# Half-size filling parcels in a stick-breaking attention mixer, and two down products in one PSUM bank

## The chip, the cores and the metric

The kernel runs on one core of one Trainium2 chip. The metric is device time of one execution in microseconds (us); lower is better. The engines are TensorE (PE, its weight loads PEld), VectorE (DVE), ScalarE (ACT), GpSimd (POOL) and SyncE (SP), which issues most loads.

## What is computed

A decoder trunk of two layers on 512 tokens with width 1024. Each layer is a half-step SwiGLU FFN (width 2816), a mixer, and a second half-step FFN, each behind an RMSNorm. Layer 0's mixer is a gated linear attention (GLA); layer 1's is stick-breaking attention with 16 heads of width 64, which the change's short name calls the softmax mixer:

```python
def sb_mixer(h, w_in, w_out):                      # per 128-query block, per head
    q, k, v = jnp.split(h @ w_in, 3, axis=-1)
    ...
        z = jnp.einsum('bhtd,bhsd->bhts', q_blk, k).astype(jnp.float32) * scale
        sp = jnp.where(mask, jax.nn.softplus(z), 0.0)
        rem = lax.cumsum(sp, axis=3, reverse=True) - sp
        weights = jnp.where(mask, jnp.exp(jax.nn.log_sigmoid(z) - rem), 0.0)
        return jnp.einsum('bhts,bhsd->bhtd', weights.astype(v.dtype), v)
    ...
    return o @ w_out
for i in range(DEPTH):
    x = x + 0.5 * swiglu(rmsnorm(x, ffn1_norm[i]), ffn1_w_gate[i], ffn1_w_up[i], ffn1_w_down[i])
    h = rmsnorm(x, mix_norm[i])
    y = gla_mixer(h, ...) if i % 2 == 0 else sb_mixer(h, ...)
    x = x + y
    x = x + 0.5 * swiglu(rmsnorm(x, ffn2_norm[i]), ffn2_w_gate[i], ffn2_w_up[i], ffn2_w_down[i])
return rmsnorm(x, final_norm)
```

## The kernel before

All activations stay on the chip, features on the 128 partitions, the 512 tokens along the free axis. Every weight is loaded as float32 (tile `raw` or `rawd`), split by ScalarE into a rounded high part `wh` (L129) and by VectorE into the rest `wl` (L130); the inputs are split in the same way. A product is then three matmuls (high by high, low by high, high by low; `mm3`, L66).

**The feed.** All weight products of the program stand in one list of entries in order (`Feed`, L140). `start()` begins the next entry; it also splits the weights of the entries that follow and issues loads up to six entries ahead. An entry's body is a generator that yields after each part of its matmuls, and `step(n)` (L161) runs n such parts. `feat` (L192) is one 128-column output block of a projection, 24 matmuls of 512 columns, and yields twice. `tok` (L211) is 256 columns of the values, 96 matmuls of 256 columns, and yields four times. `back` (L236) is the output projection of a mixer; with `late=2` its body (L269) has ten yields for each half of the output.

**The stick-breaking mixer** (`SB`, L1257; `run` L1394). Projections are queued as `pair(p)` (the query and key block of heads 2p and 2p+1, two `feat`) and `vals(c)` (256 columns of values, one `tok`): pair 0, values 0, pairs 1 and 2, values 1, pairs 3 and 4, values 2, pairs 5 and 6, values 3, pair 7, then the output projection. Pair 0 runs at the start. The heads then go through a loop of 17 rounds: round s computes the scores of head s (`weights_log`, L1309: matmuls `ps_z` L1319, then on ScalarE absolute value, exponential, logarithm and relu, on VectorE a scan and a subtraction to `r`, L1352) and turns the scores of head s-1 (`weights`, L1356: transposes `ps_T` L1366, exponential to `wt`). After the second head of a pair `values` (L1373) multiplies with the values (`ps_oT` L1381), and the result is split (`oh` L1390, `ol` L1391). Between these stand filling steps of the feed: one in `weights_log`, the others after the transposes. How many each round gets is the list `steps = [3] * 12 + [2, 1, 1, 2, 2]`. A query product is drained by `evac_q` (L1284) with two instructions on ScalarE and three on VectorE, a key product by `evac_k` (L1296) with two and seven; the first head's part stands first.

**The FFN.** Groups of columns run in a scheme with seven half-size products in place of eight (`seven`, L666, matmuls at L693); the gate product on VectorE is L706, and the copy `u` (`u3`, L736) takes one intermediate sum out of PSUM on ScalarE. Groups 1 and 3 are multiplied with the down weights by `seven_down` (L336, matmuls at L372), two parts for each group, so 16 in the program. A part's `body_1` computes products `ws`, copies them (L390), then two products `qs`, each of which is added to x by VectorE (`add`, L378), then two more pairs. `body_2` goes on with the same accumulators.

**PSUM.** There are eight banks of 512 columns. `psum()` (L47) gives a tile a bank: with a tag it takes one of that tag's banks in turn, without a tag it takes the next tag of the order `aazzztto`. All FFN products use the turn, the mixers use fixed tags. A new tile waits until the last reader of the bank's former tile has ended. A scheduler decides the order of instructions on each engine, within the dependences; each engine then works strictly in that order.

Of the kernel before, what the change touches and what calls it, by code (L numbers as in the profile page):

```python
# [21 lines left out]
KD = D // P  # L22
# [10 lines left out]
def decoder(ctx: ExitStack, tc: tile.TileContext, a: dict, out: bass.AP):  # L33
# [106 lines left out]
    class Feed:  # L140
# [18 lines left out]
            return e.body(e.W)  # L159

        def step(self, n=1, end=None):  # L161
            while n > 0:
                if self.cur is None:
                    if self.pos == end:
                        return
                    self.cur = self.start()
                if next(self.cur, self) is self:
                    self.cur = None
                else:
                    n -= 1  # L170
# [21 lines left out]
    def feat(ch, f, evac, tag=None, defer=None):  # L192


        def body(W):
            (wh, wl), = W
            ps = psum("ps_f", tag)
            for part in (range(0, KD // 2), range(KD // 2, KD)):
                for k in part:
                    mm3(ps, wh[:, k], wl[:, k], st["h"][k], st["l"][k], k == 0, k == KD - 1)  # L200
                if part[-1] == KD - 1:
                    if defer is None:
                        evac(ps)
                    else:
                        defer.append((evac, ps))
                yield

        feed.q.append(Entry([(ch, lambda t: t[:, :, f * P : (f + 1) * P], KD, P)], body))
        feed.q[-1].evac = evac

    def tok(w, c0, evac, tag=None):  # L211

        ch = Chunk(cols(w, c0, 256), KD, 256)

        def body(W):
            ps = None
            for i in range(NT):
                if i % 2 == 0:
                    ps = psum("ps_t", tag)
                o = ps[:, (i % 2) * 256 : (i % 2) * 256 + 256]  # L220
                s = slice(i * P, (i + 1) * P)
                for k in range(KD):
                    wh, wl = W[k // 4]
                    mm(o, st["h"][k][:, s], wh[:, k % 4], k == 0, False)
                    mm(o, st["h"][k][:, s], wl[:, k % 4], False, False)
                    mm(o, st["l"][k][:, s], wh[:, k % 4], False, k == KD - 1)
                if i % 2:
                    evac(i - 1, ps[:, 0:256])
                    evac(i, o)
                yield  # L230

        feed.q.append(
            Entry([(ch, (lambda t, u=u: t[:, u * 4 : u * 4 + 4]), 4, 256) for u in range(2)], body, NEAR_MOVING)
        )

    def back(w, r0, nf, hs, scale, nxt, late=0, tags=(None,) * 8):  # L236


        for dh in range(2):
            accs = []  # L240
            units = []
            for f0 in range(0, nf, 4):
                n = min(4, nf - f0)
                src = w[r0 + f0 * P : r0 + (f0 + n) * P, dh * 512 : dh * 512 + 512]
                ch = Chunk(src.rearrange("(f p) c -> p f c", p=P), n, 512)
                for u in range(0, n, 2):
                    units.append((f0 + u, (ch, (lambda t, u=u: t[:, u : u + 2]), 2, 512)))

            def done(m, dh=dh, accs=accs):
                k = dh * 4 + m  # L250
                nc.vector.scalar_tensor_tensor(
                    out=xs[k], in0=accs[m], scalar=scale, in1=xs[k], op0=ALU.mult, op1=ALU.add
                )
                if nxt is not None:
                    nxt(k)

            def acc(m, dh=dh, accs=accs):
                if m == len(accs):
                    accs.append(psum("ps_b", tags[dh * 4 + m]))
                return accs[m]  # L260

            def prod(W, u, kk, m, f, acc=acc):
                wh, wl = W[u]
                s = slice(m * P, (m + 1) * P)
                mm3(acc(m), wh[:, kk, s], wl[:, kk, s], hs[f][0], hs[f][1], f == 0, f == nf - 1)

            if nf == KD and late:

                def body(W, prod=prod, done=done):  # L269
                    for ms in ((0, 1), (2, 3)):  # L270
                        for f in range(nf - late):
                            for m in ms:
                                prod(W, f // 2, f % 2, m, f)
                            if f % 2:
                                yield
                    for m in range(4):
                        for f in range(nf - late, nf):
                            prod(W, f // 2, f % 2, m, f)
                        done(m)
                        yield  # L280

                feed.q.append(Entry([u for _, u in units], body))
                continue
            for f0, u in units:

                def body(W, f0=f0, prod=prod, done=done):
                    if f0 + 2 < nf:
                        for kk in range(2):
                            for m in range(4):
                                prod(W, 0, kk, m, f0 + kk)  # L290
                            yield
                    else:
                        for m in range(4):
                            for kk in range(2):
                                prod(W, 0, kk, m, f0 + kk)
                            done(m)
                            yield

                feed.q.append(Entry([u], body))
# [36 lines left out]
    def seven_down(pool, w, r0, hs, part):  # L336
# [43 lines left out]
        def body_1(W):  # L380
            a11, s, v["a2"] = W
            ws, zs, qs = [], [], []
            for m in range(2):
                ws.append(psum("ps_w")[:, 0:H])
                prod(ws[m], a11, 0, m, "b11", True)
            for m in range(2):


                zs.append(psum("ps_z")[:, 0:H])
                nc.scalar.copy(zs[m], ws[m])  # L390
            yield
            for m in range(2):
                qs.append(psum("ps_q")[:, 0:H])
                prod(qs[m], s, 0, m, "t1", True)
                add(m, 1, 1, qs[m])
            yield
            for m in range(2):
                prod(ws[m], s, 2, m, "t2", False)
                add(m, 0, 1, ws[m])
            yield  # L400
            for m in range(2):
                prod(zs[m], v["a2"], 0, m, "b21", False)
                add(m, 0, 0, zs[m])
            v["w"], v["q"] = ws, qs
            yield

        def body_2(W):
            (s,) = W
            ws, qs = v["w"], v["q"]

            u3 = pool().tile([P, 2, H], F32, tag="c", bufs=1, name="u3")
            for m in range(2):
                prod(ws[m], s, 0, m, "t3", False)
                nc.scalar.copy(u3[:, m], ws[m])
                add(m, 1, 1, u3[:, m])
            yield
            for m in range(2):
                prod(qs[m], s, 2, m, "b22", False)
                add(m, 0, 1, qs[m])
            yield  # L420
            for m in range(2):
                prod(ws[m], v["a2"], 2, m, "t4", False)
                add(m, 1, 0, ws[m])
            yield
# [136 lines left out]
    def two_halves(between=None):  # L561
# [2 lines left out]
        g = [feed.start(), feed.start()]  # L564
        for i in range(3):
            for x in g:
                next(x, None)
            if i == 0 and between is not None:
                between()

# [686 lines left out]
    class SB:  # L1257
# [5 lines left out]
        def __init__(self, w_in, w_out, nxt):  # L1263
# [9 lines left out]
                tok(w_in, 2 * D + c * 256, lambda i, ps: self.evac_v(c, i, ps), "z" if c == 0 else "a")  # L1273

            pair(0), vals(0), pair(1), pair(2), vals(1), pair(3), pair(4), vals(2)
            pair(5), pair(6), vals(3), pair(7)
            back(w_out, 0, KD, self.hs, 1.0, nxt, late=2, tags=("a", "a", "z", "z", "z", "t", "t", "o"))

        def evac_v(self, c, i, ps):
# [114 lines left out]
        def run(self):  # L1394
            with ExitStack() as es:
# [15 lines left out]
                exp_ln_tables(st["sqrt"])  # L1411
                flush(self.defer)
                feed.step(4)
                steps = [3] * 12 + [2, 1, 1, 2, 2]
                for s in range(17):
                    p, e = divmod(s, 2)
                    q, f = divmod(s - 1, 2)
# [1 line left out]
                    if s < 16:  # L1419
                        for i, _ in enumerate(self.weights_log(p, e)):  # L1420
                            if i == 1:
                                feed.step(1)
                                n -= 1
                    if s > 0:
                        for i, _ in enumerate(self.weights(q, f)):
                            if i < 2 and n > 0:
                                feed.step(1)
                                n -= 1
                        feed.step(n)
                        if f == 1:  # L1430
                            self.values(q)
                    else:
                        feed.step(n)
                feed.entries(self.end + 2 - feed.pos)


# [319 lines left out]
```

## Time and profile before

| what | value |
|---|---|
| times of three runs | 1834.36, 1835.29, 1831.89 us; median 1834.36 |
| profiled execution | 1833.41 us, of which the span is 1831.5 us |
| TensorE | busy 1820.1 us, 12,496 matmuls |
| VectorE, ScalarE | busy 1544.3 and 1058.7 us |
| granted TensorE clock | 0.999 of full speed |
| stick-breaking mixer's loop | about 1272 to 1462 us of the span |

Busy time counts an engine's instructions as drawn. Matmuls overlap in the drawing, so that TensorE can stand for a short while without an idle mark; the start times of matmuls that follow each other show it. In a row of waits stand the waiting engine and line, what it waited for, the total, the number and the longest. In a timeline row stand start, length, instruction, and in brackets the idle time before it and what ended it.

### The profile page before, as it was taken

Reading aid. Unit: us, or ns where it says so; the run is one execution under the profiler, and the core shown is the slowest. Engines: PE = TensorE matmul, PEld = TensorE weight load, DVE = VectorE, ACT = ScalarE, POOL = GpSimd, SP = SyncE. Lnnn points to the kernel's source line nnn. Section 1 sums busy time; section 2 is a strip of 40 time slices with the busy share of each in tenths; the row PEclk is TensorE's granted clock in tenths of the full one; section 3 lists DMA queues with packets and bytes.
Section 4 is the critical chain, followed back from the end, with each engine's and each line's share of the span. In section 5 each row is a group of like instructions: output and inputs, shape, how many; then the busy total and the mean of one; then the engine's idle time right before and its main releaser. Section 6 shows DMA issues by size and latency. Waiting matters only on the chain.

```text
span 1831.5 us, 30847 instructions
## 1 busy us (share of the span) xinstructions
PE 1820.1 (99%) x12496; PEld 1657.0 (90%) x12496; DVE 1544.3 (84%) x2529; ACT 1058.7 (58%) x1856; POOL 8.8 (0%) x20
## 2 busy tenths in 40 slices
PE   9999999999999999999999999999999999999998
PEld 7999999889888899999889999998888788999997
DVE  8999798676787989889798988976878779898886
ACT  6556555544555556555555555555878755565554
POOL 0000000000000000000000000000000000000000
PEclk9999999999999999999999999999999999999999
DMA  5433333221123333333333333322222133233331
GB/s 163 137 115 106 104 116 117 79 70 55 62 69 115 93 115 100 120 104 104 99 98 115 93 115 116 104 82 81 70 70 64 64 92 115 93 116 104 104 121 53
DMA packets 177794, 179.22 MB, mean 98 GB/s; under 512 B 4146, under 2 KB 168292, under 8 KB 177652
## 3 DMA queue, kind: packets, MB, share of 16 engines
q1 hardware_dynamic: 176800, 175.91, 30.8%
q8 instruction: 98, 1.61, 0.4%
q0 software_dynamic: 608, 1.05, 0.2%
q14 instruction: 44, 0.36, 0.1%
q10 hardware_dynamic: 244, 0.29, 0.0%
HBM read 175.17 MB, written 2.10 MB: 97 GB/s over the span
## 4 chain that ended last, share of the span: by engine, by line
PE 94%; DVE 4%; ACT 1%; DMA 1%; issue 0%; SPq 0%; DVEq 0%; ACTq 0%
PE ps_w L693 21%; PE ps_f L66 18%; PE ps_d L66 16%; PE ps_q L693 10%; PE ps_z L693 5%; PE ps_t L66 5%; PE ps_w L372 4%; PE ps_b L66 4%; PE ps_q L372 2%; PE ps_S L66 1%; PE ps_z L1319 1%; PE ps_z L372 1%; PE ps_oT L1381 1%; DVE wl L130 1%; PE ps_bt L66 1%; PE ps_T L1366 1%
## 5 line engine op out<-in xcount | busy, mean ns | idle before, releaser
L130 DVE TENSOR_TENSOR wl<-raw,wh 128x512 fp32r<-128x512 f32 (+1 forms) x242 | 256.7, 1061 | 66.8 <-ACT wh L129 47.7
L129 ACT CAST wh<-raw 128x512 fp32r<-128x512 f32 (+1 forms) x242 | 223.5, 925 | 97.7 <-PE ps_f L66 32.8
L130 DVE TENSOR_TENSOR wl<-s,wh 128x1024 fp32r<-128x1024 f32 x176 | 214.6, 1220 | 46.9 <-PE ps_z L693 29.1
L129 ACT CAST wh<-s 128x1024 fp32r<-128x1024 f32 x176 | 184.2, 1047 | 109.5 <-DVE s L683 25.1
L693 PE MATMUL ps_w<-th,wh 128*128 128x256 f32 x864 | 239.5, 277 | 1.0 <-ACT u L736 0.9
L693 PE MATMUL ps_w<-tl,wh 128*128 128x256 f32 x864 | 238.7, 276 | 0.0
L693 PE MATMUL ps_w<-th,wl 128*128 128x256 f32 x864 | 238.7, 276 | 0.0
L66 PE MATMUL ps_f<-xh,wh 128*128 128x512 f32 x432 | 172.4, 399 | 0.0
L66 PE MATMUL ps_f<-xl,wh 128*128 128x512 f32 x432 | 169.3, 392 | 0.0
L66 PE MATMUL ps_f<-xh,wl 128*128 128x512 f32 x432 | 168.9, 391 | 0.0
L693 PEld LDWEIGHTS ps_w<-th,wh 128*128 128x128 f32 x864 | 162.4, 188 | 1.8 <-ACT u L736 1.3
L66 PE MATMUL ps_d<-hh,wl 128*128 128x512 f32 x416 | 162.2, 390 | 0.0
L66 PE MATMUL ps_d<-hh,wh 128*128 128x512 f32 x416 | 162.2, 390 | 0.0
L693 PEld LDWEIGHTS ps_w<-th,wl 128*128 128x128 f32 x864 | 162.2, 188 | 0.0
L693 PEld LDWEIGHTS ps_w<-tl,wh 128*128 128x128 f32 x864 | 162.2, 188 | 0.0
L66 PE MATMUL ps_d<-hl,wh 128*128 128x512 f32 x416 | 161.8, 389 | 0.0
L129 ACT CAST wh<-rawd 128x1024 fp32r<-128x1024 f32 (+1 forms) x100 | 82.9, 846 | 71.8 <-issue 31.8
L130 DVE TENSOR_TENSOR wl<-rawd,wh 128x1024 fp32r<-128x1024 f32 (+1 forms) x100 | 96.0, 963 | 16.4 <-PE ps_z L693 8.6
L327 DVE SCALAR_TENSOR_TENSOR x<-ps_d,x 128x512 f32<-128x512 f32 x120 | 81.2, 686 | 22.9 <-PE ps_d L66 22.5
L66 PEld LDWEIGHTS ps_f<-xl,wh 128*128 128x128 f32 x432 | 81.1, 188 | 17.3
L66 PEld LDWEIGHTS ps_f<-xh,wl 128*128 128x128 f32 x432 | 81.3, 188 | 15.7
L66 PEld LDWEIGHTS ps_f<-xh,wh 128*128 128x128 f32 x432 | 81.2, 188 | 15.3
(353 smaller groups left out, 5286.1 us busy)
## 6 DMA issues: line engine op xcount, KB each, us to landing
raw<-in_ffn_w_gate_dram SPq DMA_DIRECT2D x43, 1024.0 KB, 5.4
raw<-in_ffn_w_up_dram SPq DMA_DIRECT2D x43, 1024.0 KB, 5.4
rawd<-in_ffn_w_down_dram SPq DMA_DIRECT2D x84, 512.0 KB, 3.6
raw<-in_gla_w_in_dram SPq DMA_DIRECT2D x12, 1024.0 KB, 5.3
raw<-in_sb_w_in_dram SPq DMA_DIRECT2D x16, 512.0 KB, 3.8
raw<-in_gla_w_out_dram SPq DMA_DIRECT2D x4, 1024.0 KB, 4.9
raw<-in_sb_w_in_dram SPq DMA_DIRECT2D x4, 1024.0 KB, 5.2
raw<-in_sb_w_out_dram SPq DMA_DIRECT2D x4, 1024.0 KB, 5.0
```

The lines of the kernel that those rows point to most:

```text
L66: st["pe"] = nc.tensor.matmul(ps, l, r, start=first, stop=last).ins
L129: st["cut"] = nc.scalar.copy(h[:, k], part).ins
L130: nc.vector.tensor_tensor(out=l[:, k], in0=part, in1=h[:, k].bitcast(F32), op=ALU.subtract)
L327: nc.vector.scalar_tensor_tensor(out=xs[k], in0=ps, scalar=0.5, in1=xs[k], op0=ALU.mult, op1=ALU.add)
L372: st["pe"] = nc.tensor.matmul(ps, l_, r_, start=first and c + n == 0, stop=c == 1 and n == 2, skip_group_check=True).ins
L693: st["pe"] = nc.tensor.matmul(o, l_, r_, start=first and j + n == 0, stop=j == 3 and n == 2, skip_group_check=True).ins
L1319: nc.tensor.matmul(o_, l_, r_, start=first, stop=last, skip_group_check=True)
L1366: nc.tensor.transpose(ps[:, c0 : c0 + P], ys[yb][:, yc + j * P : yc + (j + 1) * P], ident)
L1381: nc.tensor.matmul(po[e * 64 : e * 64 + 64, j * P : T], self.v[j][:, c : c + 64], self.wt[p, e][bk][:, c0 : c0 + n], start=j == 0, stop=j ...
```

## The change

Three things are changed.

1. Every body of the feed that the mixers use yields twice as often, after half as many matmuls: `feat` after two of eight input blocks, `tok` in the middle of each block of tokens, `back` after every input block (in the last parts, two yields stand together). `step(n)` runs `2 n` of these halves, so other callers get what they had; a new `halves(n)` runs single ones. `two_halves` takes two at a time.
2. In the stick-breaking mixer the values of the last block come after pair 7, and the rounds get halves: six in each of the first three, five in each of the other fourteen. The sum is 88 halves, as it was 44 steps. In a round two halves stand in `weights_log`; of five, one stands after the first transposes and two after the second.
3. In `seven_down` the two products `qs` are the halves of one bank, so one bank is asked for in place of two; only the first matmul of the first one clears the bank. The two adds stand behind both products, here and in `body_2`.

```diff
         def step(self, n=1, end=None):
+            self.halves(2 * n, end)
+
+        def halves(self, n, end=None):
             while n > 0:
...
-            for part in (range(0, KD // 2), range(KD // 2, KD)):
+            for part in (range(u, u + KD // 4) for u in range(0, KD, KD // 4)):
...
                     mm(o, st["l"][k][:, s], wh[:, k % 4], False, k == KD - 1)
+                    if k == KD // 2 - 1:
+                        yield
...
                             for m in ms:
                                 prod(W, f // 2, f % 2, m, f)
-                            if f % 2:
-                                yield
+                            yield
...
                         done(m)
+                        yield
                         yield
...
+            ps = psum("ps_q")
             for m in range(2):
-                qs.append(psum("ps_q")[:, 0:H])
-                prod(qs[m], s, 0, m, "t1", True)
+                qs.append(ps[:, m * H : (m + 1) * H])
+                prod(qs[m], s, 0, m, "t1", m == 0)
+            for m in range(2):
                 add(m, 1, 1, qs[m])
...
             for m in range(2):
                 prod(qs[m], s, 2, m, "b22", False)
+            for m in range(2):
                 add(m, 0, 1, qs[m])
...
-                next(x, None)
+                next(x, None), next(x, None)
...
-            pair(5), pair(6), vals(3), pair(7)
+            pair(5), pair(6), pair(7), vals(3)
...
-                steps = [3] * 12 + [2, 1, 1, 2, 2]
+                steps = [6] * 3 + [5] * 14
...
                             if i == 1:
-                                feed.step(1)
-                                n -= 1
+                                feed.halves(2)
+                                n -= 2
                     if s > 0:
                         for i, _ in enumerate(self.weights(q, f)):
-                            if i < 2 and n > 0:
-                                feed.step(1)
-                                n -= 1
-                        feed.step(n)
+                            if i < 2:
+                                k = min(n, n % 2 if i == 0 and n % 2 else 2)
+                                feed.halves(k)
+                                n -= k
+                        feed.halves(n)
```

More of the change, by code (lines that the diff above doesn't have):

```diff
@@ L291, in body @@
                             yield
+                            yield
                     else:
@@ L296, in body @@
                             done(m)
+                            yield
                             yield
@@ L1432, in run @@
                     else:
-                        feed.step(n)
+                        feed.halves(n)
                 feed.entries(self.end + 2 - feed.pos)
```

## The prediction

> **What bounds the kernel now.** I read the page first, then the waits of TensorE, then the timelines around each wait, then windows over the softmax mixer.
>
> ```profile
> span 1831.5 us, 30847 instructions
> PE 1820.1 (99%) x12496; PEld 1657.0 (90%) x12496; DVE 1544.3 (84%) x2529; ACT 1058.7 (58%) x1856; POOL 8.8 (0%) x20
> PE 94%; DVE 4%; ACT 1%; DMA 1%; issue 0%; SPq 0%; DVEq 0%; ACTq 0%
> ```
>
> TensorE carries 94% of the chain that ended last. The change removes no matmul, so a gain can only be time in which TensorE stood. Four rows of its waits name places that the change touches (waiting engine, for whom; total us, times, longest):
>
> ```profile
> PE ps_q L372 <- DVE o L706: 1.1, 4, 0.3
> PE ps_w L693 <- ACT u L736: 0.9, 2, 0.7
> PE ps_z L1319 <- DVE r L1352: 0.4, 2, 0.2
> PE ps_oT L1381 <- ACT wt L586: 0.2, 1, 0.2
> ```
>
> These idle times are too small, because the drawn length of a matmul overlaps the next one. The true loss is read from start to start: a 256-column matmul starts every 0.113 us, a 512-column one every 0.227 us.
>
> **1. Two products in one bank (down parts).** The first matmul of the second `ps_q` product waits.
>
> ```profile
> 254.31 0.28 PE L372 MATMUL ps_q<-hl,wh 128*128 128x256 f32 x1
> 254.88 0.38 PE L372 MATMUL ps_q<-hh,wh 128*128 128x256 f32 x1 [0.29 <-DVE o L706]
> 255.10 0.29 PE L372 MATMUL ps_q<-hh,wl 128*128 128x256 f32 x1
> ```
>
> ```profile
> 254.41 0.42 DVE L706 TENSOR_TENSOR o<-ps_w,o 128x256 f32<-128x256 f32 x1
> 256.61 0.75 DVE L378 SCALAR_TENSOR_TENSOR x<-ps_q,x 128x256 f32<-128x256 f32 x2
> ```
>
> The bank is freed at 254.41 + 0.42 = 254.83, and the matmul starts at 254.88. From 254.31 to 255.10 two starts take 0.79 us where 2 x 0.113 is due: 0.56 us lost. With both products in one bank no second bank is asked for, and the changed program has no wait on these products. Four such places: **-2.2 us**. What is late next? The two `ps_w` products behind them need the copy of `ps_w` on ScalarE:
>
> ```profile
> 254.26 0.63 ACT L390 COPY ps_z<-ps_w 128x256 f32<-128x256 f32 x2
> ```
>
> It ends at 254.89; TensorE would come to them at 255.68 - 0.56 = 255.12 (255.10 and five more starts in the trace give 255.68). It is there in time by 0.2 us. Bounds: 0 if another wait takes its place, -2.2.
>
> The adds (256.61, two in 0.75 us) now wait for both products, six matmuls or 0.68 us later. The bank is next written in the second body, behind two `ps_w`, two `ps_z` and two more `ps_w` products: 36 matmuls or 4.1 us later, so nothing on TensorE stands behind the adds. On VectorE the cuts of the next weights stand behind them; but in the row above both adds run 0.8 us after the second product's end (255.56 + 0.28), so they are late anyway and hold nobody more. I take 0 (to +10.9, rival D). The Trainium skill, "Perfetto Trace Analysis", section "Optimizing Tensor Performance", speaks against this edit: independent groups of matmuls should rotate through different banks, so that the draining of one lies beside the next. By it, the sum would grow by the waits for the adds (rival D); by the row the rotation is itself what makes TensorE wait.
>
> Each down part takes one bank fewer, so later work finds other banks. Halfway through (after 4 or 12 down parts) the rotation is shifted by four. Where layer 0's second FFN begins, its first product then falls on a bank of the mixer's output that is read late:
>
> ```profile
> 578.54 0.39 PE L66 MATMUL ps_b<-ol,wh 128*128 128x512 f32 x1
> 587.33 0.49 PE L66 MATMUL ps_R<-sh,one_r 128*128 128x512 f32 x1 [0.24 <-ACT sh L542]
> ```
>
> ```profile
> 579.03 1.88 DVE L251 SCALAR_TENSOR_TENSOR x<-ps_b,x 128x512 f32<-128x512 f32 x3
> ```
>
> The three reads end at about 579.7, 580.3 and 580.9; the FFN starts at 578.77. The changed order puts three matmuls (0.68 us) of another product ahead, so about 0.3 us is left. But 36 matmuls later TensorE waits for `sh` anyway (587.33, 0.4 us from start to start beyond a matmul), so the 0.3 us is taken from that wait: 0, at worst +0.3.
>
> **2. A copy in another place in ScalarE's queue.** The shift also changes one order in both second FFNs. Before, the copy `u` stands behind a cast that waits for VectorE:
>
> ```profile
> 660.92 1.05 ACT L129 CAST wh<-s 128x1024 fp32r<-128x1024 f32 x1 [1.59 <-DVE s L677]
> 661.88 0.36 ACT L736 COPY u<-ps_w 128x256 f32<-128x256 f32 x1
> ```
>
> ```profile
> 661.36 0.28 PE L693 MATMUL ps_q<-nl,wh 128*128 128x256 f32 x1
> 662.29 0.39 PE L693 MATMUL ps_w<-th,wh 128*128 128x256 f32 x1 [0.66 <-ACT u L736]
> 662.52 0.28 PE L693 MATMUL ps_w<-th,wl 128*128 128x256 f32 x1
> 1572.14 0.28 PE L693 MATMUL ps_q<-nl,wh 128*128 128x256 f32 x1
> 1572.66 0.38 PE L693 MATMUL ps_w<-th,wh 128*128 128x256 f32 x1 [0.24 <-ACT u L736]
> 1572.88 0.29 PE L693 MATMUL ps_w<-th,wl 128*128 128x256 f32 x1
> ```
>
> The losses are 662.52 - 661.36 - 0.23 = 0.93 us and 1572.88 - 1572.14 - 0.23 = 0.51 us. In the changed order `u` stands ahead of the cast at both places. ScalarE was idle for 1.59 us ahead of it, so `u` fits in, and the cast moves by about 0.26 us. Its product follows more than 24 matmuls (2.7 us) later. **-1.4 us**; bounds 0 and -1.4.
>
> **3. Parcels in the softmax mixer.** A step is 12 matmuls of 512 columns (or 24 of 256):
>
> ```profile
> 1429.71 0.47 PE L66 MATMUL ps_b<-oh,wh 128*128 128x512 f32 x1
> 1430.03 0.39 PE L66 MATMUL ps_b<-oh,wl 128*128 128x512 f32 x1
> 1432.54 0.39 PE L1319 MATMUL ps_z<-kh,mq 128*128 128x512 f32 x1
> 1433.07 0.39 PE L1366 MATMUL ps_T<-ident,r 128*128 128x128 f32 x2
> ```
>
> It takes 1432.54 - 1429.71 = 2.83 us: 2.72 of matmuls and about 0.1 for the change of operand kind at the first start (0.32 against 0.227). A half is 1.36 us. Before, heads 1 to 11 get three steps, the last five two, one, one, two, two; after, five halves each from head 3. Two heads (columns: stretch, length, then busy PE, PEld, DVE, ACT, POOL, clock, DMA):
>
> ```profile
> 1306.60:1331.70 25.10, 25.10 (x145) 19.79 (x143) 18.58 (x27) 20.75 (x41) 0.00 (x0) 1.00 0.21 64
> 1331.70:1356.10 24.40, 24.40 (x167) 20.44 (x166) 20.29 (x30) 19.44 (x39) 0.00 (x0) 1.00 0.23 66
> 1405.70:1429.30 23.60, 23.39 (x137) 18.09 (x135) 18.52 (x27) 21.52 (x43) 0.00 (x0) 1.00 0.13 45
> 1429.30:1441.40 12.10, 11.70 (x63) 8.55 (x62) 9.93 (x15) 11.07 (x25) 0.00 (x0) 1.00 0.27 88
> 1441.40:1461.50 20.10, 20.10 (x112) 14.71 (x112) 11.69 (x15) 13.82 (x27) 0.00 (x0) 1.00 0.10 30
> ```
>
> In the first two rows ScalarE is busy 81% and TensorE never waits: 24.75 us for two heads and six steps. In the third and fourth it is busy 91%, and there the waits for `r` and `wt` lie. What should the last three rows (55.8 us) have taken? Three pairs at 24.75 are 74.3; they hold 11 steps for 18, 7 x 2.82 = 19.7 less; the scores of a seventeenth head don't exist, an estimate of 1.5 us (0.53 from 1432.54 to 1433.07 for 1,024 columns, 2,816 in all). That leaves 53.1: **2.7 us lost at the end**. With five halves, heads 12 to 16 are no shorter than those before them, and this goes.
>
> What does it cost in heads 3 to 11, which get one half less each? A pair shrinks to 24.75 - 2.72 = 22.0 us. ScalarE's part that falls with it (100 us of the mixer, 1300 to 1400):
>
> ```profile
> L129 ACT CAST wh<-raw 128x1024 fp32r<-128x1024 f32 x12 | 12.8, 1064 | 8.3 <-DMA raw<-in_sb_w_in_dram 5.6 <-PE ps_f L66 2.7
> L1303 ACT CAST kh<-n 64x512 fp32r<-64x512 f32 x8 | 5.0, 620 | 0.1
> L1292 ACT CAST mq<-n 64x512 fp32r<-64x512 f32 x8 | 4.9, 618 | 0.2
> L1280 ACT ACTIVATE w<-ps_t,r 128x256 f32<-128x256 f32 x8 | 3.5, 504 | 0.0
> L1390 ACT CAST oh<-ps_oT 128x512 fp32r<-128x512 f32 x4 | 2.3, 586 | 6.1 <-PE ps_oT L1381 6.1
> ```
>
> 26.2 us in four pairs is 6.5 for a pair, a sixth of it 1.1. The fuller pair keeps 20.75 - 1.1 = 19.7 of 22.0 us, 89%. Idle that ScalarE cannot use, for `ps_oT`, is 6.1 / 4 = 1.5 us, so 0.8 us remains in the worst pair. Enough, but thin. One place is thinner: the key product of pair 5 now ends in the fourth half of head 9, and head 10 needs it after one half. Its drain on VectorE:
>
> ```profile
> 1424.59 0.68 DVE L1298 TENSOR_TENSOR n<-ps_f,R 128x512 f32<-128x512 f32 x1
> 1428.65 0.42 DVE L1306 CAST kl<-kl 64x512 fp32r<-64x512 f32 x1
> ```
>
> In a crowded queue the first head's half took 4.5 us from 1424.59. The changed order puts seven filling matmuls between the score matmuls there, and with one half, the transposes and these the second operand is wanted after about 3.7 us. I take +0.9 for this place and the pairs together (0 to +6), and +0.4 for four more changes of operand kind. Values last costs nothing: the last values are done with two halves of head 14 to go. SP issues that 1 MB load two loads later, behind the last pair's two; `raw` waits (5.6 us above) were hidden. Sum of this part: -2.7 + 0.9 + 0.4 = **-1.4 us**.
>
> **Sum.** -2.2 - 1.4 - 1.4 = -5.0 us. The profiled execution took 1833.4 us (span 1831.5 and 1.9 around it) and would take 1828.4. The median of the runs shown is 1834.4, 1.0 above it, so I predict **1829.4**.
>
> **Rivals.** A, the parcels even out nothing: the lost time at the end is the drain of the last heads and stays, and part 3 costs the 0.4 alone: 1834.4 - 3.6 + 0.4 = 1831.2. For it: the last head cannot be covered. Against: the rows with the waits are those with one or two steps.
>
> B, waits move: behind the `ps_q` products TensorE waits for the copy instead (its margin is 0.2 us), and `u`, a place earlier, for its input; only part 3 counts: 1833.0. Against: copy and input have ended by the rows.
>
> C, **slower**: ScalarE becomes the bound in the shortened heads. Its idle in the first two rows above, 4.35 and 4.96 us a pair, is then no slack but its own waits in order (for products, scores, loads), and stays. A pair takes 20.1 - 1.1 = 19.0 of work and 4.65 of idle, 23.7 in place of 22.0 us; over the six pairs of heads 3 to 14 that is +10.2 in place of the +0.9: 1829.4 + 9.3 = 1838.7. It starts to cost at 3.0 us of fixed idle in a pair, and the change loses from 4.0 (5.9 us over six pairs is 1.0 each). For it: 89% in the fuller pair against the 91% where waits stand. Against: only 1.5 us of the idle is waiting for a product that must come first.
>
> D, the bank: if TensorE did stand behind the adds in each of 16 down parts, 0.68 us each, +10.9 and no gain there: 1834.4 - 1.4 - 1.4 + 10.9 = 1842.5. Against: 36 matmuls lie between.
>
> **Chances.** Forecast 0.58, A 0.17, B 0.12, C 0.10, D 0.03. About 0.2% (3.7 us, so 1830.7) is what a measurement of this kernel can tell from no change. The forecast lies 1.3 us beyond it and its own spread (each part between its bounds) reaches back over it in one case of eight; A falls beyond it in four of ten. Faster 0.58, same 0.33, slower 0.09. The range holds the forecast with its parts at their better bounds (1834.4 - 2.2 - 1.4 - 2.7 less a us of spread) and A and B: 1827.0 to 1834.2. C and D are left out.
>
> **What would show it.** In the changed profile: no `ps_q` L379 wait on L717; no wait of `ps_w` L704 for `u`; a down part of 84 matmuls takes 9.5 us at all places; waits for `r` and `wt` gone after head 12; two heads of about 22 us. The prediction is wrong if TensorE waits for `wt` or for the keys in heads 3 to 12, at head 10 above all, or if the second FFNs start with a new wait.

## The result, and the profile after

| | before | changed |
|---|---|---|
| median, range, runs | 1835.23 us (1831.89 to 1836.35, 21) | 1831.37 us (1828.85 to 1833.44, 21) |
| span of the profiled execution | 1831.5 us | 1828.2 us |

The ratio is 0.998, 95% interval 0.9974 to 0.9986: 2.6 to 4.8 us faster. Forecast were -5.0 us and 1829.4.

The page of the changed kernel, in the lines that answer to those of before:

```profile
span 1828.2 us, 30828 instructions
PE 1818.1 (99%) x12496; PEld 1656.5 (91%) x12496; DVE 1543.7 (84%) x2529; ACT 1060.0 (58%) x1856; POOL 8.8 (0%) x20
PE 94%; DVE 2%; ACT 1%; DMA 1%; SPq 0%; issue 0%; DVEq 0%; ACTq 0%
```

As many matmuls as before. In TensorE's marked waits (engine, line, for whom; total us, times, longest) the four rows that the prediction began with are gone, and two new ones stand in the mixer:

```profile
PE ps_z L1330 <- ACT kh L1314: 0.5, 1, 0.5
PE ps_z L1330 <- DVE kl L1317: 0.2, 1, 0.2
```

**The down part.** TensorE's timeline at the place where 0.56 us was lost (start, length, instruction):

```profile
256.46 0.28 PE L379 MATMUL ps_q<-hl,wh 128*128 128x256 f32 x1
256.58 0.28 PE L379 MATMUL ps_q<-hh,wh 128*128 128x256 f32 x1
256.69 0.28 PE L379 MATMUL ps_q<-hh,wl 128*128 128x256 f32 x1
```

The second product (256.58) follows the first without a gap: two starts take 0.23 us, where they took 0.79.

**The copy `u`.** ScalarE's timeline in layer 0's second FFN:

```profile
662.25 0.37 ACT L747 COPY u<-ps_w 128x256 f32<-128x256 f32 x1 [1.03 <-PE ps_w L704]
662.81 1.05 ACT L129 CAST wh<-s 128x1024 fp32r<-128x1024 f32 x1 [0.19 <-DVE s L688]
```

The copy now stands ahead of the cast, and TensorE doesn't wait for it.

**The mixer's loop.** Windows whose borders are starts of matmuls: the first `ps_z` to the last `ps_oT`, then heads 9 and 10, then the end from head 12 on (stretch, length, busy PE, PEld, DVE, ACT, POOL, clock, DMA share, GB/s). First of before (loop and end):

```profile
1272.40:1461.30 188.90, 188.28 (x1137) 150.20 (x1135) 148.11 (x212) 154.92 (x310) 0.00 (x0) 1.00 0.22 67
1416.65:1461.30 44.65, 44.03 (x241) 31.97 (x239) 32.57 (x46) 36.94 (x75) 0.00 (x0) 1.00 0.18 59
```

Then of the changed kernel:

```profile
1272.35:1458.95 186.60, 185.84 (x1137) 148.78 (x1135) 148.32 (x212) 155.74 (x310) 0.00 (x0) 1.00 0.22 67
1371.81:1395.30 23.49, 22.79 (x121) 16.92 (x119) 20.08 (x30) 19.43 (x39) 0.00 (x0) 1.00 0.35 113
1404.92:1458.95 54.03, 53.98 (x343) 42.95 (x341) 37.65 (x51) 40.99 (x81) 0.00 (x0) 1.00 0.21 66
```

The loop is 2.3 us shorter. A half is six 512-column matmuls, 6 x 0.2268 = 1.361 us. The end held 16 halves and holds 25: 44.65 - 21.78 = 22.87 us beside the filling before, 54.03 - 34.03 = 20.00 after, **2.87 us less**. But heads 9 and 10 take 23.49 us where the other pairs with ten halves take 21.7 (a row with the experiment on pair 5 shows one): 1.8 us are lost there. TensorE waits for head 10's keys, at two places that take 0.76 and 0.36 us too long from start to start:

```profile
1381.45 0.48 PE L66 MATMUL ps_f<-xh,wh 128*128 128x512 f32 x1
1382.44 0.56 PE L1330 MATMUL ps_z<-kh,mq 128*128 128x384 f32 x2 [0.51 <-ACT kh L1314]
1382.84 0.40 PE L66 MATMUL ps_f<-xh,wl 128*128 128x512 f32 x1
...
1384.00 0.40 PE L66 MATMUL ps_f<-xh,wh 128*128 128x512 f32 x1
1384.59 0.44 PE L1330 MATMUL ps_z<-kl,mq 128*128 128x384 f32 x1 [0.19 <-DVE kl L1317]
```

So far the traces bear out all three gains at the places that the prediction names: -2.2, -1.4 and -2.3 us, together -5.9.

**Start by start.** Outside the mixer's loop both kernels run the same matmuls in nearly the same order, so the time from each start to the next can be compared over the whole trace. Three more stalls went, 0.8 us together: two further waits for a second `ps_q` bank (0.21 us each, at 851.8 and 1762.2 us of before), and 0.38 us at 1556.6, where TensorE waited for another copy on ScalarE (L718; its line is L729 in the changed kernel) in the same FFN as the second copy `u`. In their place eleven short breaks of 0.02 to 0.15 us are new or longer, 0.9 us together. TensorE now comes to the next products about 0.5 us sooner, and VectorE and ScalarE don't. At four places a product waits for the copy L729, of which one is, on TensorE and then on ScalarE:

```profile
276.36 0.38 PE L704 MATMUL ps_w<-th,wh 128*128 128x256 f32 x1
```

```profile
275.94 0.37 ACT L729 COPY ps_z<-ps_w 128x256 f32<-128x256 f32 x1
```

At the other seven, where a second body begins, the first weight load starts 0.05 us after the add (L385) that reads the product's bank has ended. With all this, the stalls outside the loop gave 3.5 us and the loop 2.3, so 5.8. The spans differ by 3.3, and the medians by 3.9. What takes back the rest is outside the change's own places: the first loads (1.2 us), and the pace of the matmuls (1.3).

The cast of an early load on ScalarE, first before, then changed:

```profile
23.46 1.06 ACT L129 CAST wh<-raw 128x1024 fp32r<-128x1024 f32 x1 [0.52 <-DVE t L830]
```

```profile
24.66 1.06 ACT L129 CAST wh<-raw 128x1024 fp32r<-128x1024 f32 x1 [1.70 <-DMA raw<-in_ffn_w_up_dram]
```

In the changed kernel the load landed 1.2 us later, ScalarE and VectorE run 1.2 us late until 48 us, and at 136 us TensorE is 1.16 us behind. The order of instructions is the same in both kernels up to there.

The pace: in the changed kernel's trace, 256-column matmuls start every 118 ns for 226 matmuls from 158.5, from 1056.9 and from 1631.9 us on (1.0 us each, 3.0), and no longer every 113.4. The trace of before has such stretches too, at 1154 and 1557 us (448 matmuls, 2.0 us). The granted clock is 1.00 in both.

### The profile page after: what moved, and what is told of

It is laid out like the page before. It is cut to its first block, busy times and chain, and to the rows that moved or that the text cites. A ratio compares the mean times of both kernels' runs of the same rounds, so it can differ in the third digit from the quotient of the medians.

```text
span 1828.2 us, 30828 instructions
## 1 busy us (share of the span) xinstructions
PE 1818.1 (99%) x12496; PEld 1656.5 (91%) x12496; DVE 1543.7 (84%) x2529; ACT 1060.0 (58%) x1856; POOL 8.8 (0%) x20
## 4 chain that ended last, share of the span: by engine, by line
PE 94%; DVE 2%; ACT 1%; DMA 1%; SPq 0%; issue 0%; DVEq 0%; ACTq 0%
PE ps_w L704 22%; PE ps_f L66 17%; PE ps_d L66 16%; PE ps_q L704 11%; PE ps_z L704 5%; PE ps_w L379 5%; PE ps_t L66 5%; PE ps_b L66 4%; PE ps_q L379 2%; PE ps_S L66 1%; PE ps_z L1330 1%; PE ps_z L379 1%; PE ps_oT L1392 1%; DMA raw<-in_ffn_w_up_dram 1%; PE ps_bt L66 1%; PE ps_T L1377 1%
## 5 line engine op out<-in xcount | busy, mean ns | idle before, releaser
L334 DVE SCALAR_TENSOR_TENSOR x<-ps_d,x 128x512 f32<-128x512 f32 x120 | 80.9, 686 | 21.7 <-PE ps_d L66 21.4
```

What stands on the lines that cost most here:

```text
L334: nc.vector.scalar_tensor_tensor(out=xs[k], in0=ps, scalar=0.5, in1=xs[k], op0=ALU.mult, op1=ALU.add)
```

## Experiments

The theory is the prediction's: each stall that goes brings its own length, whatever the other edits do. The rivals: the gains of the parts don't add up (waits move), the mixer's gain is the finer grain and not the evenness, and the missing 2 us are a cost of the change itself.

All medians (the runs were on several chips), with the ratio to the kernel before on the same chip, and from each trace the loop's length and the FFNs' slow matmuls (256 columns, started 116 to 122 ns after the one before, in stretches of 30 or more; 4.4 ns each):

| kernel | median us (runs) | ratio, 95% interval | loop us | slow matmuls |
|---|---|---|---|---|
| before | 1835.2 (21) | 1 | 188.87 | 448 |
| before, second trace | 1832.9 (1) | | 188.77 | 213 |
| changed | 1831.4 (21) | 0.998 (0.9974 to 0.9986) | 186.60 | 748 |
| changed, second trace | 1832.5 (11) | 0.9979 (0.9971 to 0.9988) | 186.56 | 1709 |
| one bank alone | 1830.6 (11) | 0.998 (0.9971 to 0.9989) | 188.90 | 718 |
| parcels alone | 1831.1 (11) | 0.9983 (0.9974 to 0.9992) | 186.53 | 196 |
| six, five, four halves | 1831.4 (11) | 0.9982 (0.9973 to 0.999) | 187.80 | 1053 |
| turn kept | 1830.2 (10) | 0.9973 (0.9964 to 0.9982) | 186.57 | 131 |
| halves, uneven | 1831.9 (8) | 0.9976 (0.9966 to 0.9986) | 187.05 | 1481 |
| pair 5 first | 1830.3 (5) | 0.9964 (0.9951 to 0.9978) | 184.84 | 1375 |
| pair 5 first, again | 1827.5 (5) | 0.996 (0.9947 to 0.9972) | 184.93 | 750 |
| pair 5 first, turn kept | 1828.2 (5) | 0.9962 (0.9948 to 0.9976) | 184.85 | 737 |

The loop's length is the same within 0.14 us in all traces of kernels with the same mixer. The medians can't tell 1 us; the loop can.

### One bank alone

```diff
+            ps = psum("ps_q")
             for m in range(2):
-                qs.append(psum("ps_q")[:, 0:H])
-                prod(qs[m], s, 0, m, "t1", True)
+                qs.append(ps[:, m * H : (m + 1) * H])
+                prod(qs[m], s, 0, m, "t1", m == 0)
+            for m in range(2):
                 add(m, 1, 1, qs[m])
```

> The kernel before with the shared bank alone (part 1, and with it the shifted turn of the banks and the copy's new place, part 2); parcels and the order of the values as before. The prediction's terms: -2.2 and -1.4, so -3.6 us against the kernel before (1831.6 where that takes 1835.2, ratio 0.9980); no wait of the second product for the gate product in a down part, no wait for u, and the waits for r and wt in the mixer's last heads as before. Rival B (the waits only move): within 0.5 us of before, with a new wait behind the two products. Rival D (TensorE stands behind the adds): +10.9 us.

Measured -4.1 us by the medians (interval -5.3 to -2.0). The trace has no marked wait of `ps_q` and none for `u`, and the mixer's waits as before:

```profile
PE ps_z L1322 <- DVE r L1355: 0.4, 2, 0.2
PE ps_oT L1384 <- ACT wt L589: 0.2, 1, 0.2
```

Parts 1 and 2 hold: start by start, the stalls outside the loop give -4.0 us against the first trace of before. Rival D falls, and so does B as a whole; waits did move, but only as far as the short breaks of the changed kernel, most of which are here too.

### Parcels alone

The changed kernel with that edit undone.

> The changed kernel with the two products in banks of their own again, so that only the parcels and the later values are left. The prediction's term for part 3: -1.4 us against the kernel before (ratio 0.9992); the changed kernel's trace gives -2.3 for the mixer's loop (0.9988). The waits of the second product for the gate product (four places, 2.2 us) and those for u (1.4 us) must be back. Rival A (even parcels gain nothing): +0.4 us. Rival C (ScalarE bounds the shortened heads): +6.6 us.

Its loop is 2.3 us shorter than before's, as in the changed kernel, and the waits that the bank had removed are back beside the new one at head 10:

```profile
PE ps_q L379 <- DVE o L714: 1.2, 4, 0.3
PE ps_w L701 <- ACT u L744: 0.9, 2, 0.7
PE ps_z L1327 <- ACT kh L1311: 0.5, 1, 0.5
```

The median gave -3.6 us (-4.8 to -1.5), which holds the trace's -2.3 and misses the forecast's -1.4 by 0.1. Rivals A and C fall. The medians of the two parts add up to more (7.7 us) than the whole gave (3.9), the stalls in the traces don't: -3.6 and -2.3 are the changed kernel's -5.9.

### The turn of the banks kept

```diff
             ps = psum("ps_q")
+            turn_[0] += 1
```

> The changed kernel, but the turn of the banks is moved on by one after the shared bank, so that all later tiles get the banks that they have before. The stall of the second product (2.2 us) stays away, since it is in the first one's bank; but the copy u must stand behind the waiting cast again in both second FFNs, if its place comes from the shifted turn, as the prediction has it. By the prediction: +1.4 us against the changed kernel (-2.5 against before, where the changed kernel has -3.9; ratio 0.9986), with waits for u of 0.9 and 0.5 us back. If the copy's place comes from the two products' new form and not from the turn: as the changed kernel, 0.9979.

In the trace `u` stands behind the cast again, and its wait is back; that for the gate product is not:

```profile
PE ps_w L705 <- ACT u L748: 0.9, 2, 0.7
```

So the copy's place does come from the shifted turn, and the two gains of the bank edit are separate ones. By the median, though, this kernel isn't slower than the changed one (-4.6 us, interval -6.6 to -3.3, where -2.5 was expected): it misses, and so points to something that the stalls don't hold. Its trace has the fewest slow matmuls of all. Start by start, its stalls outside the loop cost 1.6 us more than in the changed kernel's first trace, and its pace 2.6 less.

### Halves, but spread as before

```diff
-                steps = [6] * 3 + [5] * 14
+                steps = [6] * 12 + [4, 2, 2, 4, 4]
```

> The changed kernel with the filling work spread over the heads as before: six halves in the first twelve rounds, then four, two, two, four, four. Parcels of half size, the values last and the shared bank stay. If evenness is what the parcels bring (the prediction's 2.7 us of standing at the end), the gaps for r and wt after head 12 come back, the 1.1 us at head 10 goes (the key product is ready eight halves ahead), and the mixer's loop is 1.5 to 2.5 us longer than in the changed kernel: about 1833.4. If the finer grain is what gains, with two parcels to place where one stood, the loop stays within 0.7 us of the changed kernel's less the 1.1: 1830 to 1831. Rival A (the last heads' loss is a drain that no filling covers): the loop is 1.1 us shorter than in the changed kernel.

```profile
1274.22:1461.26 187.04, 186.89 (x1136) 150.00 (x1135) 148.28 (x212) 155.21 (x310) 0.00 (x0) 1.00 0.23 68
1417.93:1461.26 43.33, 43.18 (x264) 33.13 (x263) 29.43 (x39) 35.84 (x75) 0.00 (x0) 1.00 0.20 61
```

Windows of this kernel, the loop and the end from head 12 on. The loop is 0.45 us longer than the changed kernel's, between the two theories. The end shows why: 43.33 us with the 16 halves of before, so 1.3 less than before and 1.55 more than with even parcels. Of the 2.87 us, 1.3 go to the finer grain (and whatever the values' later place does) and 1.55 to evenness; the loss at head 10 is gone here, which gives 1.8 back, and one `ps_oT` group is 0.55 longer (last section): 1.55 + 0.55 - 1.8 = 0.3 of the 0.45. Neither theory alone was right.

### Six, five and four halves

```diff
-                steps = [6] * 3 + [5] * 14
+                steps = [6] * 6 + [5] * 8 + [4] * 3
```

> The changed kernel with six halves in each of the first six rounds, five in the next eight and four in the last three (the sum stays 88). The key product of pair 5 then ends three halves earlier, ahead of head 9's end. If the 1.1 us that TensorE loses at head 10 in the changed kernel is a late drain of this key product, that stall goes, and the mixer's loop takes 1.1 us less than in the changed kernel, less what the last three heads lose with four halves each (the kernel before loses 2.7 us there with 2 to 4 halves a head; 0 to 1 us): 1830.3 to 1831.3 us where before takes 1835.2. If it is instead a shortage of filling work in heads of five halves, the stall stays at head 10 or moves to another head, and the time is that of the changed kernel, 1831.4, or up to 1 us more.

The loop became 1.2 us longer. The stall for head 10's keys is gone, but at the end of the same head's round (not head 11, as a later expectation has it) TensorE loses 1.5 us from start to start, waiting for `wt`. TensorE's timeline, then ScalarE's:

```profile
1397.67 0.44 PE L1377 MATMUL ps_T<-ident,r 128*128 128x128 f32 x2 [0.62 <-ACT wt L597]
1398.04 2.15 PE L1392 MATMUL ps_oT<-wt,w 128*64 128x512 f32 x10
1400.78 0.86 PE L1392 MATMUL ps_oT<-wt,w 128*64 128x256 f32 x6 [0.58 <-ACT wt L597]
```

```profile
1397.00 1.11 ACT L597 ACTIVATE wt<-ps_T 128x512 f32<-128x512 f32 x2
1397.95 1.09 ACT L129 CAST wh<-raw 128x1024 fp32r<-128x1024 f32 x1
1399.06 1.26 ACT L1314 CAST kh<-n 64x512 fp32r<-64x512 f32 x2
1400.34 0.38 ACT L597 ACTIVATE wt<-ps_T 128x256 f32<-128x256 f32 x1
```

The last `wt` stands behind a weight cast and the key casts of the next pair, 2.3 us of casts, which now fall ahead of it. How many halves a head gets also decides where in the head a projection ends and its drain begins; evenness alone does not keep TensorE fed.

### Pair 5 ahead of the values

```diff
-            pair(0), ..., pair(3), pair(4), vals(2)
-            pair(5), pair(6), pair(7), vals(3)
+            pair(0), ..., pair(3), pair(4), pair(5)
+            vals(2), pair(6), pair(7), vals(3)
```

> The changed kernel with pair 5 (queries and keys of heads 10 and 11) ahead of the third block of values; nothing else. The key product of pair 5 then ends nine halves ahead of head 10's scores, in place of one. If the 1.1 us lost at head 10 (two gaps of 0.76 and 0.36 us) is the late drain of this product, both go and no new one comes, since the values are due only behind head 9's turn and end a half head ahead of that: the mixer's loop 1.1 us shorter than in the changed kernel, 1830.3 where that takes 1831.4. If the cause is heads that are short of filling whatever is drained in them (as the stall that went from head 10 to head 11 with six, five and four halves may mean), a gap of 0.5 to 1.5 us appears at another head, and the loop is as long as in the changed kernel.

```profile
1273.65:1458.49 184.84, 184.79 (x1137) 148.44 (x1135) 148.10 (x212) 155.47 (x310) 0.00 (x0) 1.00 0.22 68
1373.05:1394.77 21.72, 21.72 (x145) 17.70 (x143) 16.65 (x22) 18.61 (x38) 0.00 (x0) 1.00 0.35 115
```

Windows of the loop and of heads 9 and 10: 21.72 where 23.49 stood. The loop is 1.76 us shorter than in the changed kernel, no new gap comes, and TensorE is marked busy in 184.79 of 184.84 us. More than the 1.1 us expected, since the rows with waits had shown only part of what the two heads lost: 0.5 us more lay in the `ps_oT` group of pair 4 (2.80 us in the changed kernel, 2.30 here), where a matmul started 0.05 us after a `wt` that stood behind a weight cast on ScalarE, with no mark (last section). So the cause was the late drain, not a shortage of filling. By the medians it is faster than the changed kernel on the same chip too, 1830.3 us beside 1832.5, though the two intervals of the ratio overlap.

### The changed kernel and the kernel before once more

> The changed kernel once more, unaltered, for a second trace. In the first, TensorE ran 256-column matmuls at 118 ns in place of 113.4 from 158.5, 1056.9 and 1631.9 us on, for 226 matmuls each (1.0 us each). If that is decided run by run, the second trace has these stretches at other places or not at all, the sum of the time lost in them differs by a us or more between the two traces, and the spread between runs of one kernel (4.6 us) is of the same kind. If it is a property of the program, the same stretches are there again within one or two matmuls, and the kernels' differences in time hold up to 4 us of it. Time: 1831.4 us, ratio 0.998, whichever holds.

> The kernel before once more, unaltered, for a second trace of the old turn. If the shifted turn brings the slow stretches on: 450 slow 256-column matmuls in the FFNs or fewer (first trace 448, 2.0 us), none in the first FFN. If they are chance of the run: any number up to 1,700, as in the second trace of the changed kernel, and other stretches than in the first. The stalls at the down parts (four of 0.45 us and more) and for u stay, whichever holds.

The same program gave 748 and 1,709 slow matmuls (3.3 and 7.5 us), the kernel before 448 and 213. Three stretches came back within a matmul or two (158.9, 1058.7 and 1635.4 us), five others of 143 and more were new. Those 4.2 us are about the difference of the two spans, 1828.2 and 1832.3; the first loads landed 0.5 us later, and the short breaks took 0.6 us less. Between the two traces of the kernel before, the stalls outside the loop differ by 0.0 us and the loop by 0.1, but the first loads by 1.1 and the pace by 1.4. So the pace is in good part chance of the execution, and with it the spread of 4 to 5 us between executions.

Where a stretch begins shows in TensorE's timelines of the changed kernel and of the one with the turn kept, at the same product:

```profile
1056.40 0.28 PE L704 MATMUL ps_q<-tl,wh 128*128 128x256 f32 x1
1056.53 0.39 PE L704 MATMUL ps_w<-th,wh 128*128 128x256 f32 x1
1056.76 0.28 PE L704 MATMUL ps_w<-th,wl 128*128 128x256 f32 x1
1056.87 0.28 PE L704 MATMUL ps_w<-tl,wh 128*128 128x256 f32 x1
...
1057.58 0.28 PE L704 MATMUL ps_w<-tl,wh 128*128 128x256 f32 x1
```

```profile
1055.72 0.28 PE L705 MATMUL ps_q<-tl,wh 128*128 128x256 f32 x1
1055.85 0.38 PE L705 MATMUL ps_w<-th,wh 128*128 128x256 f32 x1
1056.07 0.29 PE L705 MATMUL ps_w<-th,wl 128*128 128x256 f32 x1
...
1056.31 0.28 PE L705 MATMUL ps_w<-th,wh 128*128 128x256 f32 x1
...
1056.88 0.28 PE L705 MATMUL ps_w<-tl,wh 128*128 128x256 f32 x1
```

In both, the first `ps_w` matmul comes 0.02 us late and the next 0.11. In the first, the six starts after it take 1057.58 - 1056.87 = 0.71 us, 118 ns each, and go on so for 226; in the second, five starts take 0.57, 114 ns each. Nearly the same short interruption, a wait for the copy L729 (L730), ends in one pace or the other.

### Pair 5 first with the turn kept, beside pair 5 first

> The kernel with pair 5 ahead of the values, with the turn of the banks kept as before (moved on by one after the shared bank). Slow stretches in the FFNs (256-column matmuls at 118 in place of 113.4 ns) cost 0.6 to 2.0 us in the three traces of kernels with the old turn and 3.2 to 7.5 us in the six traces with the shifted one. If the shifted turn of the banks brings them on: 131 to 450 slow matmuls here (0.6 to 2.0 us), none in the first FFN, and in spite of the 1.2 us of waits for u that come back, 1 to 4 us faster than the kernel with pair 5 first and the shifted turn. If their number is chance of the run or of the chip: as many here as in the other kernels of this call, and 1.2 us slower than the kernel with pair 5 first.

> The kernel with pair 5 ahead of the values once more, on the chip on which the one with the old turn runs. Ratio 0.9964 again by its first times (interval 0.9951 to 0.9978), no stall at head 10. If the shifted turn brings the slow stretches on: at least 700 slow matmuls in the FFNs (3 us), one stretch of them in the first FFN. If they are chance: any number.

By then the kernels with the old turn had shown 131 to 448 slow matmuls and those with the shifted one 718 to 1,709, as if the change itself cost 3 us of pace. As a rule that fell: 737 with the old turn, a stretch at 158 us in the first FFN among them, and 750 with the shifted one, none in the first FFN. The kernel with the turn kept was 0.7 us slower, in ranges that nearly coincide (1826.9 to 1830.4 and 1826.0 to 1829.5), so the waits for `u`, which are back in its trace, can't be told from this time. The turn alone doesn't decide the pace. Whether it shifts its mean stays open: 1.5 us in the five traces with the old turn, 4.9 in the seven with the shifted one, one execution each. Only the 737 lies above any of the seven (718), which speaks for the turn; but the three highest counts come from one chip, on which no kernel with the old turn was traced.

## Why the prediction was right, and where it was off

- **Part 1, -2.2: right at the four places, not in what it put at nothing.** Of the down parts at 254, 703, 1151 and 1613 us, the changed kernel's trace takes 0.53, 0.57 and 0.56 us less in three, and 0.80 in one that the slow pace had lengthened. Two more places, which the prediction left out, gave 0.4. But "nothing on TensorE stands behind the adds" is wrong: at seven places TensorE's next weights wait for the adds, and at four its products wait for the copy L729, 0.9 us together. All in all this part came to about -1.8. The bank that is read late at the start of layer 0's second FFN was forecast well: 0.39 us lost there, 0.45 won back at the wait for `sh`.
- **Part 2, -1.4: right**, with its cause: the wait for `u` goes with the shifted turn and comes back with the old one. With the 0.38 us lost just ahead of the second `u`, at 1556.6, it gave -1.8: those two stalls together cost 0.9 us in all five traces with the old turn and are gone with the shifted one.
- **Part 3, -1.4: -2.3 measured.** The loss at the end was 2.87 for 2.7 forecast. The step mis-sized was "+0.9 for this place and the pairs together": the place was head 10, as named, and TensorE's wait for the keys there is what the prediction had set down as a sign that it is wrong; it cost 1.8 us with the wait for `wt` beside it. A term was missing the other way. "TensorE never waits" was read from the marks, but the `ps_oT` groups of pairs 1 and 3 each held 0.6 us of unmarked waiting for `wt`, which is gone (last section). -2.87 + 1.8 - 1.2 = -2.3, and the loop has -2.27, so nothing is left for the "+0.4" of changes of operand kind.
- **What the evenness does** was half right: a bit over half of the gain at the end.
- **The sum, -5.0:** the stalls give -5.8, the time -3.9 (-4.8 to -2.6), the second series -4.1 (-5.3 to -2.2). The forecast lies just outside the first interval and inside the second. That it came so near is luck in part: the places brought more than reckoned, and 1 to 3 us don't arrive. In the pair of traces 1.2 of them are the landing of the first loads and 1.3 the pace; both vary as much between two executions of the kernel before. Whether a slower pace goes with the change on average stays open.
- **Values last, 0:** not tried alone. With even parcels they can't stand ahead of pair 7: its keys would end at the 76th half, and head 14 begins after 73.

## What to carry to other kernels

When filling work is spread evenly over stages, reckon where each projection's last product falls and what its drain stands in front of: the order of the entries (pair 5 ahead of the values) brought 1.8 us, while the two other counts of parcels that were tried lost more elsewhere. Where single terms of 1 us are at stake in a time that varies by 4, measure the stage between two of its own matmuls, here the same within 0.14 us, and only then the whole. A bank rotation can make a wait of its own: two products in one bank removed it, since nothing needed the bank for 36 matmuls. But a stall that goes brings less than its length when the next inputs are only just in time: here 2.7 us went and 0.9 came back in small breaks. And a list of marked waits is not the whole loss; the start times are.

## What the hardware showed

**Two paces at a granted clock of 1.00.** Stretches of 256-column matmuls run at 118 ns in place of 113.4, 3.9% slower. In the FFNs of the twelve traces there are 53 of them: 49 begin at a short break in the flow (as above), and 47 last until 512-column matmuls follow. They cost 0.6 to 7.5 us a trace. What decides the pace after a break stays open; a kernel without such breaks was not run.

**A wait without a mark: two 64-column products side by side.** The sixteen `ps_oT` matmuls of a pair of heads, eight for each head (each head fills one half of the bank's partitions), take several lengths. Before, for pair 1, on TensorE and then on ScalarE:

```profile
1328.81 2.94 PE L1381 MATMUL ps_oT<-wt,w 128*64 128x512 f32 x16
1331.68 0.44 PE L1319 MATMUL ps_z<-kh,mq 128*128 128x384 f32 x1
```

```profile
1328.29 1.27 ACT L1303 CAST kh<-n 64x512 fp32r<-64x512 f32 x2
1329.59 0.87 ACT L586 ACTIVATE wt<-ps_T 128x512 f32<-128x512 f32 x2
```

Changed, for the same pair:

```profile
1326.02 2.37 PE L1392 MATMUL ps_oT<-wt,w 128*64 128x512 f32 x16
1328.32 0.45 PE L1330 MATMUL ps_z<-kh,mq 128*128 128x384 f32 x1
```

```profile
1326.86 0.38 ACT L597 ACTIVATE wt<-ps_T 128x256 f32<-128x256 f32 x1
1327.96 1.26 ACT L1314 CAST kh<-n 64x512 fp32r<-64x512 f32 x2 [0.72 <-DVE n L1309]
```

Changed, all sixteen start as eight pairs of equal length, one matmul of each head, 6 or 7 ns within a pair. Before, only the four of 512 columns do. One head's matmuls run on at the same times, but the other's first one of 384 columns starts at 1330.24, 0.05 us after the `wt` that it reads has ended (the first of the two in the row, at 1330.19), and all that follow it are late: 2.87 us from the first to the next `ps_z` in place of 2.30. It is a wait for ScalarE, where the key casts of the next pair stood ahead of this `wt`; in the changed kernel they come after the last `wt`. No mark shows it, since TensorE was busy with the other head's matmuls meanwhile. In the twelve traces all sixteen whole groups of more than 2.33 us have such a matmul, 0.05 to 0.06 us after a `wt`. The Trainium skill, "TensorEngine Tiling (Array Packing)", section "Key Properties", has it that different tiles of the array can run matmuls in parallel; the 6 to 7 ns agree, and so does one head's going on while the other waits.
